# Two decoder layers on one core: list order on every engine and a fixed matmul sequence in the feed-forward part

## The chip, the cores and the metric

The kernel runs on one core of a Trainium2 chip. The metric is the device time of one execution in microseconds (us), lower is better; a timing is the median of several executions. The engines have short names in the views: PE is TensorE (matmuls), PEld its weight loads, DVE is VectorE, ACT is ScalarE, POOL is GpSimd and SP is SyncE, which here only starts DMAs. PEclk is the TensorE clock that was granted, as a share of 2.4 GHz.

## The reference

The trunk has two layers over 512 positions of width 1024, in fp32. Cut to what matters:

```python
for i in range(DEPTH):
    h = rmsnorm(x, mix_pre_g[i])
    z = h @ w_in[i]                   # columns for three mixers
    out_a = spatial_gating(...)       # causal chunks of 128
    out_b = silu(r_g) * retention(...)  # 6 heads, rotary
    out_c = forgetting_attention(...) # 6 heads, log_sigmoid(f_f + fox_b_f[i])
    x = x + rmsnorm(concat(out_a, out_b, out_c) @ w_o[i], mix_post_g[i])

    h = rmsnorm(x, ffn_pre_g[i])
    g = h @ w_gate[i]                 # 1024 x 4096
    conv = conv_b + sum(shift(g, 2 - j) * conv_w[j] for j in range(3))
    f = (gelu(conv) * (h @ w_up[i])) @ w_down[i]
    x = x + rmsnorm(f, ffn_post_g[i])

    gate = sigmoid(rmsnorm(x, ple_pre_g[i]) @ w_ple_gate[i])
    x = x + rmsnorm((p[i] @ w_ple_proj[i]) * gate, ple_post_g[i])
```

## The kernel before

Every fp32 product is made of three fp32r matmuls: each operand is split into a high and a low part (`split`: ScalarE casts the high part, VectorE subtracts it to get the low part), and TensorE adds high x high, high x low and low x high in one bank of its accumulator memory (`mm3`).

No instruction is issued where it is written. A class `Plan` records each operation with what it depends on and what it costs; `issue` then simulates the engines with those costs and with delays between engines, and so makes a list, `order`. The loop at its end (line 404, the line that every row of the profile bears) issues the operations in that order. The framework's own scheduler then orders each engine's queue, and may take operations in another order than the list's. `SETS` says how many places of 8 KB per partition the tiles of two kinds have: X for fp32r operands such as activations, W for the split feed-forward weights; raw weights (`graw`, `ws`) have no kind and go where a place is left (`pick`).

At the program's start x comes in four chunks of 128 positions. Per chunk VectorE multiplies x by the gain in two halves (`h`), TensorE transposes (`hps`), ScalarE and VectorE split the transposed tile (`hT`), and TensorE projects it (`ps`) on weights that come as `traw` and are split to `thl`.

The feed-forward part has 32 blocks of 128 columns per layer. In a block, `gate_up(b)` loads four weight pieces (`graw`: u1, u2 of w_up and g1, g2 of w_gate, one for each half of the inner dimension), makes sums of them, splits pieces and sums (`wg`, `wsa`, `wsb`, `wu`) and makes seven products in the manner of Winograd: b11 and b21 on `wg`, h6 and d on `wsa`, h7 and b22 on `wsb`, h4 on `wu`. Each is 12 matmuls of 128x256 into the banks `beta` or `ag`, and after each product ScalarE or VectorE moves the bank's values into `gs` or `us`. The convolution (`cv`), gelu and the gate follow, and a split into `act`. From block 4 on the down projection of the four blocks before is made meanwhile: 24 matmuls of 128x512 per block (`dn`), in two passes of 12, each ending in an add into `facc`. In blocks 28 to 31 there are 1, 2, 2 and 3 passes.

`down` (line 1126) is written after the whole of `gate_up` in a block, but matmuls depend only on their data, so the order of `dn` and products on TensorE follows from the list and the framework.

Of the kernel before, what the change touches and what calls it, by code (L numbers as in the profile page):

```python
# [28 lines left out]
F32R = mybir.dt.float32r  # L29
# [20 lines left out]
class Plan:  # L50
# [7 lines left out]

    SETS = {"X": 18, "W": 6}

# [7 lines left out]

    def __init__(self):
        self.ops = []  # L70
        self.table = {}
        self.tiles = {}
        self.real = {}
        self.fenced = False
        self.kind = {}
        self.place = {}
        self.scratch = bacc.Bacc("TRN2", target_bir_lowering=False, num_devices=1)

    def fence(self):

        self.fenced = True

    def pool(self, pool, psum=False):
# [63 lines left out]
    def record(self, engine, fn, method, args, kw):  # L147
# [23 lines left out]
        if engine == "PE":  # L171
            if self.fenced:
                deps.add(self.newest)
            self.newest, self.fenced = i, False
            t = self.tiles[outs[0].tensor.name]
            if len(t) > 6:
                deps.add(t[6])
            t[6:] = [i]
        self.ops.append((engine, fn, args, kw, deps, used, self.cost(engine, method, outs, ins, args, kw)))

    def cost(self, engine, method, outs, ins, args, kw):
# [13 lines left out]
        if engine == "PE":  # L195
# [3 lines left out]
            if dt == F32R:  # L199
                return 0.4416 * n + 6, 0, n * rows  # L200
            half = 0.5 if kw["lhsT"].shape[0] == 64 or kw["lhsT"].shape[-1] == 64 else 1
# [19 lines left out]
    def issue(self):  # L221
# [56 lines left out]
        def pick(t):  # L278
# [5 lines left out]
            spare, c = max(room, default=(0, None))  # L284
            return c if spare > 0 else None

# [72 lines left out]
        while len(order) < n:  # L359
# [39 lines left out]
            while finish and finish[0][0] <= now:  # L399
                _, i = heapq.heappop(finish)  # L400
                complete(i, now)
        for i in order:
            o = ops[i]
            o[1](*[self.map(v) for v in o[2]], **{k: self.map(v) for k, v in o[3].items()})  # L404

# [41 lines left out]
def packed(w):  # L447
# [16 lines left out]
    for g, u in zip(w["w_gate"], w["w_up"]):  # L464
        g, u = (blocks(m).reshape(-1, P, 2, 512) for m in (g, u))
        gu.append(np.stack([u[:, :, 1], g[:, :, 0], g[:, :, 1], u[:, :, 0]], 2))
    r["gu"] = gu
# [7 lines left out]
def body(ctx, tc, a, out):  # L475
    nc = tc.nc
    plan = Plan()
    V, A, G, T, SY = (plan.engine(n, e) for n, e in (
# [579 lines left out]
    def ffn(l, hs, emb, x, new, g, nxt):  # L1058
# [15 lines left out]

        def gate_up(b):
            raw = b8("graw", (2048,))
            load(raw, a["w_gu"][l, b].rearrange("p s n -> p (s n)"))
            u2, g1, g2, u1 = (raw[:, i * 512:i * 512 + 512] for i in range(4))
            wg = b8("wg", (2, 1024), F32R)
            split(wg[:, 0, :], wg[:, 1, :], raw[:, 512:1536])  # L1080
            s = b8("ws", (2048,))
            V.tensor_tensor(out=s[:, 512:1536].rearrange("p (s n) -> p s n", s=2), in0=raw[:, 0:1024].rearrange("p (s n) -> p s n", s=2),
                            in1=u1.unsqueeze(1).to_broadcast([P, 2, 512]), op=ALU.add)
            V.tensor_tensor(out=s[:, 0:512], in0=s[:, 1024:1536], in1=u2, op=ALU.add)
            sa = b8("wsa", (2, 1024), F32R)
            split(sa[:, 0, :], sa[:, 1, :], s[:, 0:1024])
            V.tensor_tensor(out=s[:, 1536:2048], in0=s[:, 0:512], in1=g2, op=ALU.add)
            sb = b8("wsb", (2, 1024), F32R)
            split(sb[:, 0, :], sb[:, 1, :], s[:, 1024:2048])
            wu = [wk("wu", dt=F32R) for _ in range(2)]  # L1090
            split(wu[0], wu[1], u2)

            beta, ag = bank("beta"), bank("ag")
# [16 lines left out]
            product(ga, part(sb, 1), "b22", False, True)  # L1110
            V.tensor_tensor(out=gs[:, t2], in0=ga, in1=gs[:, t2], op=ALU.add)
            product(be, wu, "h4", False, True)
            A.mul(us[:, t1], be, -1.0)

# [10 lines left out]

        def down(q, c, u):

            ps = bank("dn")
            ts = slice(c * P, c * P + P)
            for j in range(4):  # L1130
                t = acts[2 * q + j // 2]
                mm3(ps, lambda i: t[:, i, j % 2, ts], lambda i: u(i, j), j == 0, j == 3)
            return ps

        def wd(q, hf):
            return tm_units(a["w_dn"][l, q, hf], 512, 4)

        embed(l, *emb)
        for b in range(32):
            gate_up(b)  # L1140
            q, i = divmod(b, 4)
            if not q:
                continue
            i0, i1 = ((0, 2, 4, 6, 8) if q < 7 else (0, 1, 3, 5, 8))[i:i + 2]
            for hf, c in [divmod(j, 4) for j in range(i0, i1)]:
                if c == 0:
                    u = wd(q - 1, hf)
                ps = down(q - 1, c, u)
                if q == 1 and hf == 0 and c % 2 == 0:
                    facc.append(b8("facc", (2, D)))  # L1150
                fr = facc[c // 2][:, c % 2, hf * 512:hf * 512 + 512]
                if q == 1:
                    A.copy(fr, ps)
                else:
                    V.tensor_tensor(out=fr, in0=ps, in1=fr, op=ALU.add)

# [3 lines left out]
        for c in range(NCH):  # L1160
            fr = facc[c // 2][:, c % 2, :]
            parts = []
            for hf in range(2):
                ps = down(7, c, us[hf])
                cs = slice(hf * 512, hf * 512 + 512)
                V.tensor_tensor(out=fr[:, cs], in0=ps, in1=fr[:, cs], op=ALU.add)
                parts.append(post_part(fr[:, cs], g[:, 0, cs], fr[:, cs]))
# [137 lines left out]
```

## Time and profile before

| what | value |
|---|---|
| median of the 3 runs shown | 1635.08 us (1634.15 to 1640.05) |
| profiled execution | 1635.78 us |
| its span | 1633.7 us |
| its mean granted TensorE clock | 0.995 |
| TensorE busy, matmuls | 1594.8 us (98%), 10034 |
| VectorE busy | 1239.0 us (76%) |
| ScalarE busy | 840.0 us (51%) |
| GpSimd busy | 93.7 us (6%) |

The span is the time from the first to the last instruction of the profiled execution. Busy time is the time in which an engine executes, and a matmul counts as executing until its result is out, so that neighbours in a pipeline overlap; the distance between the starts of two runs of matmuls, divided by the number of matmuls, gives their true spacing.

### The profile page before, as it was taken

Reading aid. Unit: us, or ns where it says so; the run is one execution under the profiler, and the core shown is the slowest. Engines: PE = TensorE matmul, PEld = TensorE weight load, DVE = VectorE, ACT = ScalarE, POOL = GpSimd, SP = SyncE. Lnnn points to the kernel's source line nnn. Section 1 sums busy time; section 2 is a strip of 40 time slices with the busy share of each in tenths; the row PEclk is TensorE's granted clock in tenths of the full one; section 3 lists DMA queues with packets and bytes.
Section 4 is the critical chain, followed back from the end, with each engine's and each line's share of the span. In section 5 each row is a group of like instructions: output and inputs, shape, how many; then the busy total and the mean of one; then the engine's idle time right before and its main releaser. Section 6 shows DMA issues by size and latency. Waiting matters only on the chain. (4 is left out here: it accounts for less than half of the span.)

```text
span 1633.7 us, 25124 instructions
## 1 busy us (share of the span) xinstructions
PE 1594.8 (98%) x10034; PEld 1409.9 (86%) x10034; DVE 1239.0 (76%) x1949; ACT 840.0 (51%) x1378; POOL 93.7 (6%) x157
## 2 busy tenths in 40 slices
PE   6999999999999999999999999999999999999998
PEld 5887687999999999998888776879999999999987
DVE  6466758988788788786774568599788788788784
ACT  5335626765554554554562346386554554555453
POOL 1000011000000000001230000110000000000022
PEclk8999999999999999999999999999999999999999
DMA  8213216323323324336543033172334233234441
GB/s 295 91 65 104 101 69 228 108 94 114 110 78 124 104 78 129 100 99 261 192 165 104 27 129 121 49 258 78 104 104 129 78 104 129 78 104 130 179 157 65
DMA packets 63421, 197.48 MB, mean 121 GB/s; under 512 B 7348, under 2 KB 15164, under 8 KB 63304
## 3 DMA queue, kind: packets, MB, share of 16 engines
q1 hardware_dynamic: 63160, 195.81, 35.5%
q8 instruction: 79, 1.29, 0.3%
q14 instruction: 38, 0.31, 0.1%
q10 hardware_dynamic: 144, 0.07, 0.0%
HBM read 178.52 MB, written 17.33 MB: 120 GB/s over the span
## 5 line engine op out<-in xcount | busy, mean ns | idle before, releaser
L404 PE MATMUL dn<-thl,act 128*128 128x512 f32 x1536 | 368.0, 390 | 0.0
L404 PEld LDWEIGHTS dn<-thl,act 128*128 128x128 f32 x1536 | 282.8, 188 | 54.0
L404 PE MATMUL ps<-thl,hT 128*128 128x512 f32 (+3 forms) x984 | 206.5, 368 | 0.1
L404 PEld LDWEIGHTS ps<-thl,hT 128*128 128x128 f32 x984 | 177.7, 190 | 22.8 <-ACT hT L404 0.5
L404 DVE TENSOR_TENSOR thl<-traw,thl 128x1024 fp32r<-128x1024 f32 (+2 forms) x120 | 141.2, 1185 | 37.2 <-ACT thl L404 36.4
L404 ACT CAST thl<-traw 128x1024 fp32r<-128x1024 f32 (+2 forms) x120 | 121.0, 1020 | 50.6 <-PE fps L404 10.7
L404 PE MATMUL beta<-hb,wg 128*128 128x256 f32 x768 | 104.7, 281 | 4.6 <-DVE wg L404 4.6
L404 PEld LDWEIGHTS beta<-hb,wg 128*128 128x128 f32 x768 | 100.6, 189 | 9.3 <-DVE wg L404 5.0
L404 ACT COPY gs<-beta 128x256 f32<-128x256 f32 x128 | 47.6, 372 | 111.4 <-PE beta L404 111.3
L404 PE MATMUL ag<-hb,wg 128*128 128x256 f32 x768 | 103.0, 283 | 0.0
L404 PE MATMUL beta<-hh,wsa 128*128 128x256 f32 x768 | 101.7, 282 | 0.5 <-DVE wsa L404 0.2
L404 PE MATMUL beta<-hh,wu 128*128 128x256 f32 x768 | 102.0, 282 | 0.1
L404 PE MATMUL beta<-hh,wsb 128*128 128x256 f32 x768 | 101.8, 281 | 0.0
L404 PE MATMUL ag<-hd,wsa 128*128 128x256 f32 x768 | 100.8, 281 | 0.9 <-DVE gs L404 0.9
L404 PEld LDWEIGHTS beta<-hh,wu 128*128 128x128 f32 x768 | 94.0, 188 | 8.8 <-DVE us L404 7.3
L404 DVE TENSOR_TENSOR wsa<-ws,wsa 128x1024 fp32r<-128x1024 f32 x64 | 78.2, 1221 | 30.8 <-ACT wsa L404 25.7
L404 PE MATMUL ag<-hb,wsb 128*128 128x256 f32 x768 | 100.8, 280 | 0.0
L404 PEld LDWEIGHTS beta<-hh,wsa 128*128 128x128 f32 x768 | 95.4, 190 | 1.4 <-ACT gs L404 0.6
L404 PEld LDWEIGHTS ag<-hb,wg 128*128 128x128 f32 x768 | 96.3, 191 | 0.0
L404 PEld LDWEIGHTS ag<-hd,wsa 128*128 128x128 f32 x768 | 94.8, 189 | 1.7 <-DVE gs L404 1.3
L404 DVE SCALAR_TENSOR_TENSOR cv<-gs,cw,cv 128x511 f32<-128x511 f32 (+1 forms) x128 | 95.4, 745 | 0.9
L404 PEld LDWEIGHTS beta<-hh,wsb 128*128 128x128 f32 x768 | 94.5, 189 | 1.7 <-ACT gs L404 1.2
(194 smaller groups left out, 2709.1 us busy)
## 6 DMA issues: line engine op xcount, KB each, us to landing
graw<-in_w_gu_dram SPq DMA_DIRECT2D x128, 512.0 KB
traw<-in_w_dn_dram SPq DMA_DIRECT2D x64, 512.0 KB
x<-x SPq DMA_DIRECT2D x40, 512.0 KB
fraw<-in_w_fm_dram SPq DMA_DIRECT2D x30, 512.0 KB
traw<-in_w_wo_dram SPq DMA_DIRECT2D x16, 512.0 KB
traw<-in_w_pg_dram SPq DMA_DIRECT2D x16, 512.0 KB
x<-in_x_dram SPq DMA_DIRECT2D x8, 512.0 KB
traw<-in_w_uv_dram SPq DMA_DIRECT2D x8, 512.0 KB
```

The source lines that it names most:

```text
L404: o[1](*[self.map(v) for v in o[2]], **{k: self.map(v) for k, v in o[3].items()})
```

## The change

Six things change.

1. `SETS` goes from X 18 and W 6 to X 15 and W 9, and `pick` lets the oldest raw tile have a place at once.
2. `fence(True)` makes each matmul depend on the one recorded before it. It holds in the feed-forward part from block 4 to block 30, so TensorE's sequence is there the written one.
3. The cost of an fp32r matmul in the plan goes from 0.4416 n + 6 to 0.4427 n nanoseconds for n columns.
4. `issue` gives each operation a dependency without a semaphore on the operation issued before it on the same engine, so every engine, SP and GpSimd too, keeps the list's order.
5. The four weight pieces are stored in the order u2, u1, g1, g2. `wg` and `wu` are split first; then the sums are made in place in `graw` by four adds of 512 columns. Before, three adds (one of 1024 columns and two of 512) wrote to a tile of their own, `ws`. That is one 8 KB tile less and one VectorE instruction more in each of 64 blocks.
6. In a block's written order, 22 of the 24 `dn` matmuls stand between the products b22 and h4, and the last two stand after h4, at the block's end. `down` gives these two back as `rest`.

The number of matmuls stays the same, and so do the loads.

```diff
-    SETS = {"X": 18, "W": 6}
+    SETS = {"X": 15, "W": 9}
...
-    def fence(self):
+    def fence(self, always=None):
 
         self.fenced = True
+        if always is not None:
+            self.strict = always
 
...
-            if self.fenced:
+            if self.fenced or self.strict:
                 deps.add(self.newest)
...
-                return 0.4416 * n + 6, 0, n * rows
+                return 0.4427 * n, 0, n * rows
...
-            return c if spare > 0 else None
+            return c if spare > 0 or first[t] <= front else None
...
+        newest = {}
         for i in order:
             o = ops[i]
-            o[1](*[self.map(v) for v in o[2]], **{k: self.map(v) for k, v in o[3].items()})
+            made = o[1](*[self.map(v) for v in o[2]], **{k: self.map(v) for k, v in o[3].items()})
+            if o[0] in newest:
+                self.tc.add_manual_dep(made.ins, newest[o[0]], mybir.DependencyInfo(mybir.DependencyClass.NoSync, mybir.DependencyReason.DATA), reason="order of the plan")
+            newest[o[0]] = made.ins.name
...
-        gu.append(np.stack([u[:, :, 1], g[:, :, 0], g[:, :, 1], u[:, :, 0]], 2))
+        gu.append(np.stack([u[:, :, 1], u[:, :, 0], g[:, :, 0], g[:, :, 1]], 2))
...
-        def gate_up(b):
+        def gate_up(b, between):
             raw = b8("graw", (2048,))
             load(raw, a["w_gu"][l, b].rearrange("p s n -> p (s n)"))
-            u2, g1, g2, u1 = (raw[:, i * 512:i * 512 + 512] for i in range(4))
+            u2, u1, g1, g2 = (raw[:, i * 512:i * 512 + 512] for i in range(4))
             wg = b8("wg", (2, 1024), F32R)
-            split(wg[:, 0, :], wg[:, 1, :], raw[:, 512:1536])
-            s = b8("ws", (2048,))
-            V.tensor_tensor(out=s[:, 512:1536].rearrange("p (s n) -> p s n", s=2), in0=raw[:, 0:1024].rearrange("p (s n) -> p s n", s=2),
-                            in1=u1.unsqueeze(1).to_broadcast([P, 2, 512]), op=ALU.add)
-            V.tensor_tensor(out=s[:, 0:512], in0=s[:, 1024:1536], in1=u2, op=ALU.add)
-            sa = b8("wsa", (2, 1024), F32R)
-            split(sa[:, 0, :], sa[:, 1, :], s[:, 0:1024])
-            V.tensor_tensor(out=s[:, 1536:2048], in0=s[:, 0:512], in1=g2, op=ALU.add)
-            sb = b8("wsb", (2, 1024), F32R)
-            split(sb[:, 0, :], sb[:, 1, :], s[:, 1024:2048])
+            split(wg[:, 0, :], wg[:, 1, :], raw[:, 1024:2048])
             wu = [wk("wu", dt=F32R) for _ in range(2)]
             split(wu[0], wu[1], u2)
+            for t, by in ((g1, u1), (u1, u2), (u2, g1), (g2, u2)):
+                V.tensor_tensor(out=t, in0=t, in1=by, op=ALU.add)
+            sa = b8("wsa", (2, 1024), F32R)
+            split(sa[:, 0, :], sa[:, 1, :], raw[:, 0:1024])
+            sb = b8("wsb", (2, 1024), F32R)
+            split(sb[:, 0, :], sb[:, 1, :], raw[:, 1024:2048])
 
...
             product(ga, part(sb, 1), "b22", False, True)
             V.tensor_tensor(out=gs[:, t2], in0=ga, in1=gs[:, t2], op=ALU.add)
+            rest = between()
             product(be, wu, "h4", False, True)
+            if rest:
+                rest()
             A.mul(us[:, t1], be, -1.0)
...
-        def down(q, c, u):
+        def down(q, c, u, done):
 
             ps = bank("dn")
             ts = slice(c * P, c * P + P)
             for j in range(4):
                 t = acts[2 * q + j // 2]
-                mm3(ps, lambda i: t[:, i, j % 2, ts], lambda i: u(i, j), j == 0, j == 3)
-            return ps
+                for i, (h, r) in enumerate(((0, 0), (0, 1), (1, 0))):
+                    if j < 3 or not i:
+                        T.matmul(ps, lhsT=t[:, h, j % 2, ts], rhs=u(r, j), start=j == 0 and i == 0, stop=False)
+
+            def rest():
+                T.matmul(ps, lhsT=t[:, 0, 1, ts], rhs=u(1, 3), start=False, stop=False)
+                T.matmul(ps, lhsT=t[:, 1, 1, ts], rhs=u(0, 3), start=False, stop=True)
+                done(ps)
+            return rest
 
         def wd(q, hf):
             return tm_units(a["w_dn"][l, q, hf], 512, 4)
 
-        embed(l, *emb)
-        for b in range(32):
-            gate_up(b)
+        units = {}
+
+        def pieces(b):
+
             q, i = divmod(b, 4)
             if not q:
-                continue
+                return None
+            rest = None
             i0, i1 = ((0, 2, 4, 6, 8) if q < 7 else (0, 1, 3, 5, 8))[i:i + 2]
             for hf, c in [divmod(j, 4) for j in range(i0, i1)]:
                 if c == 0:
-                    u = wd(q - 1, hf)
-                ps = down(q - 1, c, u)
+                    units[q, hf] = wd(q - 1, hf)
                 if q == 1 and hf == 0 and c % 2 == 0:
                     facc.append(b8("facc", (2, D)))
-                fr = facc[c // 2][:, c % 2, hf * 512:hf * 512 + 512]
-                if q == 1:
-                    A.copy(fr, ps)
-                else:
-                    V.tensor_tensor(out=fr, in0=ps, in1=fr, op=ALU.add)
+
+                def add(ps, fr=facc[c // 2][:, c % 2, hf * 512:hf * 512 + 512]):
+                    if q == 1:
+                        A.copy(fr, ps)
+                    else:
+                        V.tensor_tensor(out=fr, in0=ps, in1=fr, op=ALU.add)
+                if rest:
+                    rest()
+                rest = down(q - 1, c, units[q, hf], add)
+            return rest
+
+        embed(l, *emb)
+        for b in range(31):
+            if b == 4:
+                plan.fence(True)
+            gate_up(b, lambda: pieces(b))
+        plan.fence(False)
+        gate_up(31, lambda: None)
+        pieces(31)()
 
...
-                ps = down(7, c, us[hf])
                 cs = slice(hf * 512, hf * 512 + 512)
-                V.tensor_tensor(out=fr[:, cs], in0=ps, in1=fr[:, cs], op=ALU.add)
+                down(7, c, us[hf], lambda ps: V.tensor_tensor(out=fr[:, cs], in0=ps, in1=fr[:, cs], op=ALU.add))()
```

How the instructions move shows in the order on the engines' queues; xN is a number of like instructions in a row.

VectorE at the program's start, before. `h` is x times the gain, two per chunk; `thl` 128x1024 is the split of the first weights, `thl` 128x2x390 that of the `fv` weights, `hT` the low part of the transposed h.

```order
L404 TENSOR_TENSOR h<-x,gain 128x512 x2
L404 TENSOR_TENSOR thl<-traw,thl 128x1024
L404 TENSOR_TENSOR hT<-hps,hT 128x4x128 x2
L404 TENSOR_TENSOR thl<-traw,thl 128x1024 x3
L404 TENSOR_TENSOR thl<-traw,thl 128x2x390 x2
L404 TENSOR_TENSOR h<-x,gain 128x512 x5
L404 TENSOR_TENSOR hT<-hps,hT 128x4x128 x3
L404 TENSOR_TENSOR h<-x,gain 128x512
L404 TENSOR_TENSOR hT<-hps,hT 128x4x128 x2
```

The same place on VectorE with the change:

```order
L408 TENSOR_TENSOR h<-x,gain 128x512 x2
L408 TENSOR_TENSOR thl<-traw,thl 128x1024
L408 TENSOR_TENSOR hT<-hps,hT 128x4x128 x2
L408 TENSOR_TENSOR thl<-traw,thl 128x1024 x3
L408 TENSOR_TENSOR h<-x,gain 128x512 x5
L408 TENSOR_TENSOR hT<-hps,hT 128x4x128 x3
L408 TENSOR_TENSOR h<-x,gain 128x512
L408 TENSOR_TENSOR hT<-hps,hT 128x4x128 x2
L408 CAST ang<-posi 128x512
L408 TENSOR_SCALAR ang<-ang,invf 128x512
L408 TENSOR_SCALAR angn<-ang 128x512
L408 TENSOR_TENSOR hT<-hps,hT 128x4x128
```

The two splits of the `fv` weights stood ahead of the five `h` and now stand behind these rows.

TensorE in one block of layer 1's feed-forward part, before, from the product b11 (`hb` on `wg`) to the block's last `dn`:

```order
L404 MATMUL beta<-hb_2154,wg 128x256 x12
L404 MATMUL ag<-hb_2169,wg 128x256 x12
L404 MATMUL beta<-hh_2239,wsa 128x256 x12
L404 MATMUL ag<-hd,wsa 128x256 x12
L404 MATMUL beta<-hh_2248,wsb 128x256 x12
L404 MATMUL ag<-hb_2228,wsb 128x256 x12
L404 MATMUL dn<-thl,act 128x512 x2
L404 MATMUL beta<-hh_2266,wu 128x256 x12
L404 MATMUL dn<-thl,act 128x512 x22
```

The same in each block with the change:

```order
L408 MATMUL beta<-hb_2154,wg 128x256 x12
L408 MATMUL ag<-hb_2169,wg 128x256 x12
L408 MATMUL beta<-hh_2237,wsa 128x256 x12
L408 MATMUL ag<-hd,wsa 128x256 x12
L408 MATMUL beta<-hh_2252,wsb 128x256 x12
L408 MATMUL ag<-hb_2275,wsb 128x256 x12
L408 MATMUL dn<-thl,act 128x512 x22
L408 MATMUL beta<-hh_2295,wu 128x256 x12
L408 MATMUL dn<-thl,act 128x512 x2
```

The run of 22 `dn` and the run of two have changed places around the seventh product; before, other blocks had other runs at other places, and now all from 4 to 27 are alike.

ScalarE ahead of layer 1's output projection, before. `fet` is a copy of transposed attention weights out of `tps`, `rr` a step of the same mixer, the casts to `thl` are splits of weights, those to `ehl` and `cc` other operands.

```order
L404 COPY fet<-tps 128x4x128
L404 ACTIVATE rr<-rps 32x512
L404 CAST thl<-traw 128x1024
L404 COPY rr<-rps 32x512
L404 ACTIVATE rr<-rps 32x512
L404 COPY rr<-rps 32x512
L404 CAST thl<-traw 128x1024
L404 COPY fet<-tps 128x4x128
L404 CAST ehl<-eraw 128x1024
L404 CAST cc<-ops 128x512
```

The same place on ScalarE with the change:

```order
L408 COPY fet<-tps 128x4x128
L408 ACTIVATE rr<-rps 32x512
L408 COPY rr<-rps 32x512
L408 COPY fet<-tps 128x4x128
L408 ACTIVATE rr<-rps 32x512
L408 COPY rr<-rps 32x512
L408 CAST cc<-ops 128x512
L408 CAST thl<-traw 128x1024 x6
```

The casts of weights have moved behind both copies to `fet`.

## Rows read from the trace of the kernel before

**Rows 1.** The page: busy time, share of the span and instructions of each engine.
```profile
PE 1594.8 (98%) x10034; PEld 1409.9 (86%) x10034; DVE 1239.0 (76%) x1949; ACT 840.0 (51%) x1378; POOL 93.7 (6%) x157
```

**Rows 2.** Windows, three stretches: the two at the start, then blocks 5 to 27.
```profile
core 0: us, PE busy (x) PEld busy (x) DVE busy (x) ACT busy (x) POOL busy (x), PEclk, DMA share, GB/s
17.70:25.50 7.80, 0.01 (x1) 0.01 (x1) 2.60 (x4) 4.84 (x7) 0.79 (x2) 0.68 0.98 306
25.50:30.00 4.50, 4.50 (x21) 4.50 (x22) 4.50 (x7) 3.09 (x5) 1.18 (x1) 0.50 1.01 395
335.80:691.00 355.20, 355.14 (x2486) 329.95 (x2485) 291.46 (x386) 186.26 (x283) 0.00 (x0) 1.00 0.31 101
```

**Rows 3.** Timeline of PE, blocks 5 and 6: start, duration, group, idle before and releaser.
```profile
336.10 1.58 PE L404 MATMUL beta<-hb,wg 128*128 128x256 f32 x12
...
340.34 0.39 PE L404 MATMUL dn<-thl,act 128*128 128x512 f32 x1
340.57 1.53 PE L404 MATMUL ag<-hd,wsa 128*128 128x256 f32 x12
...
346.01 5.40 PE L404 MATMUL dn<-thl,act 128*128 128x512 f32 x23
351.25 1.58 PE L404 MATMUL beta<-hb,wg 128*128 128x256 f32 x12
...
359.73 0.63 PE L404 MATMUL dn<-thl,act 128*128 128x512 f32 x2
360.20 1.53 PE L404 MATMUL beta<-hh,wu 128*128 128x256 f32 x12
361.56 5.17 PE L404 MATMUL dn<-thl,act 128*128 128x512 f32 x22
```

**Rows 4.** Timeline of PE, the first product of block 28.
```profile
691.32 1.58 PE L404 MATMUL beta<-hb,wg 128*128 128x256 f32 x12
```

**Rows 5.** Timeline of DVE at the program's start.
```profile
12.84 2.35 DVE L404 TENSOR_TENSOR thl<-traw,thl 128x1024 fp32r<-128x1024 f32 x2
22.78 2.06 DVE L404 TENSOR_TENSOR thl<-traw,thl 128x780 fp32r<-128x780 f32 x2 [7.59 <-ACT thl L404]
24.75 3.54 DVE L404 TENSOR_TENSOR h<-x,gain 128x512 f32<-128x512 f32 x5
...
30.61 1.27 DVE L404 TENSOR_TENSOR hT<-hps,hT 128x512 fp32r<-128x512 f32 x2
```

**Rows 6.** Timeline of ACT at the program's start.
```profile
13.38 1.06 ACT L404 ACTIVATE junk<-x 128x1024 bf16<-128x1024 f32 x1 [0.15 <-DMA x<-in_x_dram]
...
19.77 1.05 ACT L404 ACTIVATE junk<-x 128x1024 bf16<-128x1024 f32 x1
...
21.90 0.84 ACT L404 CAST thl<-traw 128x780 fp32r<-128x780 f32 x1 [0.99 <-DMA traw<-in_w_fv_dram]
```

**Rows 7.** Timeline of PE at the program's start.
```profile
25.49 4.53 PE L404 MATMUL hps<-k_ident,h 128*128 128x128 f32 x20 [7.83 <-DVE h L404]
29.67 1.92 PE L404 MATMUL ps<-thl,hT 128*128 128x512 f32 x5
```

**Rows 8.** Timeline of PE, the end of a later block.
```profile
406.11 0.39 PE L404 MATMUL dn<-thl,act 128*128 128x512 f32 x1
406.47 1.66 PE L404 MATMUL beta<-hh,wu 128*128 128x256 f32 x12
407.96 5.40 PE L404 MATMUL dn<-thl,act 128*128 128x512 f32 x23
```

**Rows 9.** Lines of DVE, blocks 5 to 27: count, busy us, mean ns, idle before.
```profile
L404 DVE TENSOR_TENSOR ws<-ws,graw 128x512 f32<-128x512 f32 x46 | 31.6, 687 | 0.8
...
L404 DVE TENSOR_TENSOR ws<-graw 128x1024 f32<-128x1024 f32 x22 | 26.8, 1218 | 0.3
```

**Rows 10.** Timeline of PE, the first products of layer 1's feed-forward part.
```profile
278.62 1.42 PE L404 MATMUL beta<-hb,wg 128*128 128x256 f32 x10 [2.28 <-DVE wg L404]
```

**Rows 11.** Timeline of PE ahead of layer 1's output projection.
```profile
204.38 2.37 PE L404 MATMUL ops<-fet,mix 128*64 128x512 f32 x14 [1.78 <-ACT fet L404]
```

**Rows 12.** Timeline of PE, the same place in layer 2.
```profile
1008.30 2.37 PE L404 MATMUL ops<-fet,mix 128*64 128x512 f32 x14 [2.06 <-ACT fet L404]
```

More of the change, by code (lines that the diff above doesn't have):

```diff
@@ L67, with __init__ @@
     HOP_PE = {"PE": 0, "DVE": 250, "ACT": 270, "POOL": 190, "SP": 100}
-    def __init__(self):
+    def __init__(self, tc):
+        self.tc = tc
         self.ops = []
@@ L73, in __init__ @@
         self.real = {}
-        self.fenced = False
+        self.fenced = self.strict = False
         self.kind = {}
@@ L476, in body @@
     nc = tc.nc
-    plan = Plan()
+    plan = Plan(tc)
     V, A, G, T, SY = (plan.engine(n, e) for n, e in (
```

## The prediction

> **What bounds the kernel now.** I read the page first. TensorE is busy for 98% of the span, VectorE for 76% [rows 1]. A busy share that high can still hide time, because a matmul that is spaced more widely than it need be counts as busy. So the next view was the windows, by stage: at the program's start TensorE stands idle from 17.70 to 25.50 and then runs 4.5 us at a granted clock of 0.50, the lower of its two levels (1.2 GHz); in blocks 5 to 27 of layer 1's feed-forward part it is busy for 355.14 of 355.20 us at clock 1.00 [rows 2]. The bound of the feed-forward part is therefore TensorE's own spacing of matmuls, and the third view, the timeline with start times, shows that spacing.
>
> In the timeline of the feed-forward part a run's start is exact enough to divide by. Block 5 starts at 336.10 and block 28 at 691.32 [rows 3, 4]: 355.22 / 23 = **15.44 us per block**. Inside, the same 128x256 matmul has two spacings. After one `dn` matmul at 340.34, 48 of them take 340.57 to 346.01, 113.3 ns each; after 23 `dn`, 72 take 351.25 to 359.73, 117.8 ns each; after two `dn` again, 12 take 360.20 to 361.56, 113.3 ns [rows 3]. All are at clock 1.00 and nothing waits. Over both layers I found 20 runs of one or two `dn` with no wait behind them, and all are followed by the 113 ns spacing; 54 runs of twelve or more `dn` are all followed by 118 ns. I don't know the mechanism; I take the regularity as it stands.
>
> **The start: list order on VectorE.** Now VectorE ends the splits of the first weights at 12.84 + 2.35 = 15.19, then idles 7.59 us, because the split of the `fv` weights stands next in its queue, and those land late: ScalarE starts on them at 21.90, released by their DMA [rows 5, 6]. Behind it stand five `h` (x times gain), which TensorE's transposes need; its idle time ends on them at 25.49, and chunk 1's projection starts at 29.67 [rows 7]. The x that they read was there: ScalarE reads chunk 1 at 13.38, and the last chunk at the latest at 19.77 [rows 6]. After the change the five `h` stand ahead of that split. They run from 15.19 for 3.54 us to 18.7, two low parts of hT add 1.27, so the projection starts near 20.0: 29.67 − 20.0 = 9.7 us earlier. The lower bound is the idle time alone, 7.6. I take **−9**: the transposes, now 4.53 us at the lower clock, come after a shorter pause, but the DMA engines are 98% busy in that stretch [rows 2], and later weights may not keep pace.
>
> **The feed-forward part: where the `dn` stand.** The new block runs six products, 22 `dn`, the seventh product and two `dn`. By the regularity the six products follow a run of two and the seventh a run of 22: 72 x 113.3 ns = 8.16, 12 x 117.8 = 1.41, and 24 `dn` at (351.25 − 346.01) / 23 = 227.8 ns = 5.47. Sum **15.04 us** against 15.44: −0.40 x 23 = −9.2 per layer. Blocks 28 to 31 also begin behind a run of two: 4 x 72 x 4.5 ns = −1.3. Two layers: **−21**.
>
> Part of that is not spacing. In 12 blocks per layer the seventh product waits for its weights `wu`, which VectorE splits last: 406.11 to 406.47 is 0.36 for one `dn`, 0.13 too much, and the product takes 1.49, where 12 x 117.8 would be 1.41 and 12 x 113.3 is 1.36 [rows 8]; in all 0.21 to 0.26 us, about 5 us over 24 blocks. After the change `wu` is split ahead of the sums and has 22 `dn`, 5 us, in front of its product, so these waits should go. The other 16 are spacing.
>
> The Trainium skill, "TensorE: Matmul & The Clock Gate", section "Back-to-back issue gap", gives the isolated gap of a warm matmul as set by its column count alone, N/2.4 + 2.5 ns with 262 cycles for N = 256; by it the order of runs would change nothing. The trace disagrees, with 113.3 and 117.8 ns for one shape [rows 3]; by the page this term would keep only its 5 us of waits.
>
> **The price of a fixed sequence.** Now the scheduler may put a `dn` where a product's operand isn't ready, as at 340.34 between `wsa` and `d` [rows 3]. After the change nothing can be put there: a product that waits holds all behind it, 24 `dn` and the next block's products. At each of four boundaries a ScalarE or VectorE step that drains the bank must fit under the product between. Such a step has 12 x 113.3 = 1.36 us now instead of 1.41. The trace has no row of a fixed sequence; below, the price is nothing, above it is one wait of 0.21 at each of four boundaries in 28 blocks of two layers, 0.21 x 4 x 56 = +47. I take **+2**, near the lower end, because in block 5's neighbour (351.25 to 359.73) six products already run in that sequence without a gap.
>
> **Sums in place.** Per block one add of 1218 ns and two of 687 [rows 9] make 2.59 us; four of 687 make 2.75, +0.16. VectorE is busy 291.46 / 23 = 12.67 us per block [rows 2], then 12.83 of 15.04: 2.2 us stay free, and that hides it. Without that cover it would be 0.16 x 64 = 10 us. The sums now stand behind the splits of `wg` and `wu`, so `wsa` comes later relative to its load, while one 8 KB tile per block is saved. At a layer's entry the first `wg` product waits 2.28 us on VectorE's split [rows 10]; `wg` no longer stands behind the adds, `wsa` does. I take **0**, bounds −4.6 and +4.6: the 2.28 us gone or doubled in both layers.
>
> **List order elsewhere, tile sets.** In the mixers the output projection waits 1.78 and 2.06 us on a ScalarE copy `fet` [rows 11, 12], ahead of which the old queue has casts of weights; the new queue has both `fet` copies first. **−3**, bounds 0 and −3.8. SP's loads, too, now go in list order: a load that waits for its buffer holds the later ones, while the DMA engines are 31% busy in the feed-forward part [rows 2], which hides some delay. Three fewer X places and three more W places, the cost constants and POOL's order have no row; I take 0, bounds −6 and +6: the two mixer waits and the entry wait (1.78 + 2.06 + 2.28) saved or met once more.
>
> **Sum.** −9 − 21 + 2 − 3 = −31. The profiled execution took 1635.8 us (span 1633.7), 0.7 over the median of the runs shown, so 1604.8 by it and 1604.1 by the median: I say **1605**.
>
> **Rivals.**
> A: the spacing doesn't follow the last run of `dn` but something that goes along with it in the old order, such as which product comes next. For it: I have no mechanism. Against: 20 of 20 and 54 of 54. Then the 16 us of spacing stay: **1621**.
> B: the start is gained and lost again, because the `fv` weights and those after them land no earlier and TensorE waits for them instead. For it: the DMA engines are 98% busy before 25.5 [rows 2], and `fv` lands at 21.90 [rows 6]. Against: the first weights are split by 15.19 [rows 5], and three more chunks can be projected on them. Then −9 becomes 0: **1614**.
> C (slower): waits at the boundaries of the fixed sequence. For it: VectorE has but 2.2 us per block free, and its work comes in bursts. With 0.21 us at all four boundaries the time is 1605 − 2 + 47 = **1650**. It decides from 40 us on, 0.7 us per block in 56 blocks: then the time is over 1643.
> D: list order helps in more places of the mixers and at the layers' entries, since other queues too hold a late load's split ahead of ready work. Both lower bounds above, −6 and −4.6: **1594**.
> E: no net change, by the mechanism of C at two or three of the four boundaries: 0.21 x 2.5 x 56 = 29 us eat the gains, **1632**. That the change doesn't do what it says is excluded by the rows of the order shown with the change.
>
> **How the numbers follow.** The forecast as summed has 0.48, A 0.13, B 0.12, C 0.06, D 0.15, E 0.06. A difference under 0.5%, 8.2 us, can't be told from none. The range goes from D's value, 1594, to just above A, 1622; outside stand C, E and the half of D that gains more than its value, 0.2 in all. The likeliest case alone, with small errors in its four terms, has 1598 to 1612. Faster by over 0.5% (under 1626.9) are the forecast, A, B and D: 0.88; the same is E, 0.06; slower is C, 0.06.
>
> **What would show it.** Right: block starts 15.0 us apart; 113 ns in six products and 118 in the seventh; no wait ahead of `wu`; VectorE's gap of 7.6 us at the start gone and the projection near 20; the `fet` wait under 0.5. Wrong: 118 ns in all products (A); a gap on `fv` or `fm` weights before 60 us (B); repeated gaps of 0.2 us ahead of `h6`, `h7` or `b22` named on ScalarE or VectorE (C). The forecast rests above all on two matmuls of `dn` at a block's end setting the spacing of the next 72.

## The result and the profile after

The changed kernel takes 1615.36 us (median of 4 runs, 1614.30 to 1617.16) against 1636.64 for the kernel before in the same comparison: a ratio of 0.987, 95% interval 0.9847 to 0.9892. That is 21 us less where 31 were forecast. The profiled execution took 1614.30 us, its span is 1612.5, its granted clock 0.998.

The page of the changed kernel, busy time by engine:

```profile
PE 1577.5 (98%) x10034; PEld 1393.0 (86%) x10034; DVE 1240.0 (77%) x2013; ACT 840.5 (52%) x1380; POOL 92.0 (6%) x157
```

TensorE's share is 98% as before [rows 1], with the same 10034 matmuls in 17 us less: they lie closer together. VectorE has the 64 instructions more and hardly more busy time.

To see where the time went I cut both traces at the starts of the same matmuls: the first `sps` (attention scores), the first `wo` (output projection), the first `beta` (feed-forward part) and the last `dn` of each layer. Each length is the distance between two such starts, the first one from the start of the span; the last column is an experiment told below.

| stage, us | before | changed | X 18, W 6 |
|---|---|---|---|
| program start to `sps` | 74.1 | 64.0 | 64.9 |
| `sps` to `wo`, layer 1 | 126.2 | 129.7 | 127.0 |
| `wo` to `beta`, layer 1 | 75.4 | 76.0 | 75.4 |
| `beta` to last `dn`, layer 1 | 501.2 | 489.6 | 490.1 |
| last `dn` to `wo`, layer 2 | 227.0 | 230.4 | 227.8 |
| `wo` to `beta`, layer 2 | 75.7 | 76.0 | 75.4 |
| `beta` to last `dn`, layer 2 | 500.6 | 492.3 | 490.5 |
| last `dn` to last matmul | 46.1 | 47.0 | 46.1 |

The changed kernel gains 10.0 us at the start and 11.6 + 8.3 = 19.9 in the two feed-forward parts, and gives back 3.5 and 3.4 in the two stages with attention, 0.8 around the output projections and 0.9 at the end: 8.6 in all.

The changed kernel's timeline of VectorE at the program's start:

```profile
15.14 3.10 DVE L408 TENSOR_TENSOR h<-x,gain 128x512 f32<-128x512 f32 x5
...
20.54 1.29 DVE L408 TENSOR_TENSOR hT<-hps,hT 128x512 fp32r<-128x512 f32 x2
```

Where it idled 7.59 us [rows 5], the five `h` now start at 15.14, right behind the splits of the first weights. On TensorE one chunk's projection on the first weights is 24 matmuls `ps`. Before, chunk 0's ran without a break, and TensorE then stood idle up to 25.49 [rows 7]:

```profile
9.87 7.80 PE L404 MATMUL ps<-thl,hT 128*128 128x512 f32 x24
```

In the changed kernel the transposes of the later chunks stand among them:

```profile
9.90 6.50 PE L408 MATMUL ps<-thl,hT 128*128 128x512 f32 x17
16.25 0.60 PE L408 MATMUL hps<-k_ident,h 128*128 128x128 f32 x4
16.60 0.48 PE L408 MATMUL ps<-thl,hT 128*128 128x512 f32 x1
...
19.05 2.33 PE L408 MATMUL ps<-thl,hT 128*128 128x512 f32 x9
```

Behind the 17 come three single ones (16.60, 17.71, 18.38) and four of the nine; the 25th, with which chunk 1 begins, starts at 20.07 where it was 29.67 [rows 7]. A view of the trace from 20.24 on, when chunk 0's last one has ended, begins with it:

```profile
20.07 1.31 PE L408 MATMUL ps<-thl,hT 128*128 128x512 f32 x5
```

The changed kernel's timeline of TensorE from there on, in the order of time:

```profile
194.17 2.37 PE L408 MATMUL ops<-fet,mix 128*64 128x512 f32 x14
...
212.73 0.66 PE L408 MATMUL cps<-k_ident,ro 128*128 128x128 f32 x4 [1.07 <-DVE ro L408]
...
224.09 0.63 PE L408 MATMUL cps<-k_ident,ro 128*128 128x128 f32 x4 [0.61 <-DVE ro L408]
...
271.95 1.42 PE L408 MATMUL beta<-hb,wg 128*128 128x256 f32 x10 [1.78 <-DVE wg L408]
...
277.17 0.50 PE L408 MATMUL beta<-hh,wsa 128*128 128x256 f32 x2 [1.65 <-ACT wsa L408]
...
328.95 1.53 PE L408 MATMUL beta<-hb,wg 128*128 128x256 f32 x12
...
359.33 1.53 PE L408 MATMUL beta<-hb,wg 128*128 128x256 f32 x12
...
367.50 5.17 PE L408 MATMUL dn<-thl,act 128*128 128x512 f32 x22
372.51 1.58 PE L408 MATMUL beta<-hh,wu 128*128 128x256 f32 x12
373.92 0.63 PE L408 MATMUL dn<-thl,act 128*128 128x512 f32 x2
374.39 1.53 PE L408 MATMUL beta<-hb,wg 128*128 128x256 f32 x12
...
675.59 1.53 PE L408 MATMUL beta<-hb,wg 128*128 128x256 f32 x12
...
1565.10 0.97 PE L408 MATMUL ps<-thl,hT 128*128 128x512 f32 x3 [1.72 <-DVE thl L408]
```

Read it from the middle. A block runs from 359.33 to 374.39, 15.06 us: six products in 367.50 − 359.33 = 8.17, 113.5 ns a matmul, and the seventh, behind 22 `dn`, in 373.92 − 372.51 = 1.41, 117.5 ns. Over blocks 5 to 27 it is (675.59 − 328.95) / 23 = 15.07 us against 15.44 [rows 3, 4]. At the entry the wait on `wg`, 2.28 [rows 10], is 1.78, and a wait of 1.65 on `wsa` has come behind it. The wait on `fet` [rows 11] is gone (194.17), but some 19 and 30 us later the projection's neighbours `cps` wait 1.07 and 0.61 on `ro`. At 1565.10, in the last embedding stage, a wait of 1.72 on weights is new.

What no wait shows is the loss between `sps` and `wo`. TensorE has 128.55 us of work in 129.6 there, and its idle time is 0.7 us less than before. Grouped by shape, the attention's matmuls that fill only half of the array (64 rows for the scores `sps`, 64 columns for `ops`) have the same counts and more busy time. (A shape in a row names the rows and columns of the array, then the result; one such matmul of the program is two records in the trace, which accounts for the counts.) Lines of PE between `sps` and `wo` of layer 1, before: count, busy us, mean ns, idle before.

```profile
L404 PE MATMUL sps<-fqk 64*128 64x384 f32 x12 | 3.4, 508 | 0.0
L404 PE MATMUL ops<-fet,mix 128*64 128x512 f32 x10 | 3.4, 618 | 0.1
L404 PE MATMUL sps<-fqk 64*128 64x512 f32 x12 | 3.2, 606 | 0.0
...
L404 PE MATMUL ops<-fet,mix 128*64 128x384 f32 x8 | 1.8, 486 | 0.0
```

And the same lines of the changed kernel:

```profile
L408 PE MATMUL ops<-fet,mix 128*64 128x512 f32 x10 | 5.4, 618 | 0.3 <-ACT fet L408 0.3
L408 PE MATMUL sps<-fqk 64*128 64x512 f32 x12 | 4.4, 624 | 0.0
L408 PE MATMUL sps<-fqk 64*128 64x384 f32 x12 | 4.2, 500 | 0.0
L408 PE MATMUL ops<-fet,mix 128*64 128x384 f32 x8 | 3.3, 499 | 0.0
```

One matmul takes as long as before (618 ns for `ops` 128x512, before and after), but the group covers 5.4 us instead of 3.4: the matmuls overlap less. The starts tell why. Two `sps` 64x384 side by side alternate: their starts lie 6, 316, 7 and 316 ns apart, 645 ns for both. Where another matmul stands between the two, the one by itself takes 323 + 412 = 735 ns. The new order on TensorE has such places (here a shape is that of the result in the program, so that `ops` 64x512 is the pair of records 128x512 above):

```
L408 MATMUL fps<-hT,fhl 128x512
L408 MATMUL ops<-fet,mix_414 64x512
L408 MATMUL fps<-hT,fhl 128x512 x2
L408 MATMUL ops<-fet,mix_414 64x512
L408 MATMUL ops<-fet,mix_414 64x384 x2
```

Before, the two `ops` 64x512 stood in one row of the order, and so did both `sps` of a pair with 384 columns. Summed from each start to the next matmul's start, `ops` and `sps` take 14.3 us in this stage before and 18.1 after. The difference of 3.8 covers the stage's loss of 3.5. Between the layers, in the next attention, they take 15.4 and 18.1: 2.7 of the 3.4 lost there.

### The profile page after: what moved, and what is told of

Its sections match the earlier page's. It is cut to its first block, busy times and chain, and to the rows that moved or that the text cites. A ratio compares the mean times of both kernels' runs of the same rounds, so it can differ in the third digit from the quotient of the medians.

```text
span 1612.5 us, 25222 instructions
## 1 busy us (share of the span) xinstructions
PE 1577.5 (98%) x10034; PEld 1393.0 (86%) x10034; DVE 1240.0 (77%) x2013; ACT 840.5 (52%) x1380; POOL 92.0 (6%) x157
## 5 line engine op out<-in xcount | busy, mean ns | idle before, releaser
L408 DVE TENSOR_TENSOR graw<-graw 128x512 f32<-128x512 f32 x256 | 176.3, 690 | 2.7
L408 PEld LDWEIGHTS beta<-hh,wu 128*128 128x128 f32 x768 | 98.3, 189 | 6.1 <-DVE us L408 1.9
L408 PE MATMUL beta<-hb,wg 128*128 128x256 f32 x768 | 99.8, 278 | 3.6 <-DVE wg L408 3.6
L408 DVE TENSOR_TENSOR wg<-graw,wg 128x1024 fp32r<-128x1024 f32 x64 | 78.3, 1224 | 28.0 <-PE beta L408 17.7
L408 PE MATMUL beta<-hh,wsa 128*128 128x256 f32 x768 | 98.2, 277 | 1.7 <-ACT wsa L408 1.6
L408 DVE TENSOR_TENSOR wsb<-graw,wsb 128x1024 fp32r<-128x1024 f32 x64 | 78.3, 1224 | 27.2 <-PE beta L408 18.2
L408 PE MATMUL beta<-hh,wsb 128*128 128x256 f32 x768 | 98.2, 277 | 0.0
```

Source lines behind the costliest of these rows:

```text
L408: made = o[1](*[self.map(v) for v in o[2]], **{k: self.map(v) for k, v in o[3].items()})
```

## The experiments

Every comparison is against the kernel before on the same chip; its median was 1636.3 in the first two groups of four and 1633.8 in the third (X 18, W 6 with the old cost; the sums with X 18, W 6; the run without the fixed sequence; the last one). The changed kernel itself ran beside a kernel before of 1636.6, so against the third group the ratios are the fairer measure.

**Where the last down matmuls stand.** Three kernels change one number, how many `dn` are left for a block's end (`TAIL` is 0, 3 or 4 in place of 2; the code is cut):

```diff
-                    if j < 3 or not i:
+                    if 3 * j + i < 12 - TAIL:
...
             def rest():
-                T.matmul(ps, lhsT=t[:, 0, 1, ts], rhs=u(1, 3), start=False, stop=False)
-                T.matmul(ps, lhsT=t[:, 1, 1, ts], rhs=u(0, 3), start=False, stop=True)
+                for m in range(12 - TAIL, 12):
+                    ...
```

None:

> All 24 down matmuls of a block stand ahead of the seventh product, none at the block's end. Theory (the last run of down matmuls sets the spacing): the six products that follow have 118 ns, 72 x 4.5 ns = 0.32 us more per block, in some 54 blocks +17.5 us: 1633. Rival (the place in the block, or which product it is, sets the spacing): 113 ns stay in six products, 1615 as the changed kernel.

Three:

> Three instead of two down matmuls at a block's end. The trace of the changed kernel has four runs of three, each followed by 113 ns, so the theory says 113 ns in six products and 1615, within 2 us. Rival (two is special): 118 ns and 1633.

Four:

> Four down matmuls at a block's end. The trace of the changed kernel has two runs of four, each followed by 60 matmuls at 118 ns. Theory (a run long enough loses the short spacing, and four is long enough): 118 ns in all products, 1633. Rival (any tail at the block's end will do, and those two places were something else): 1615.

Measured: none 1632.24 us (ratio to before 0.9973, 0.9964 to 0.9983), three 1617.83 (0.9883, 0.9864 to 0.9902), four 1635.33 (0.9991, 0.9980 to 1.0001). All three are nearest to what the theory said and far from the rival, though not exactly: three came 2.8 us over its 1615, where 2 had been allowed, and four 2.3 over its 1633. The timelines of TensorE in one block, first with none at the end:

```profile
405.63 1.58 PE L408 MATMUL beta<-hh,wu 128*128 128x256 f32 x12
407.05 1.58 PE L408 MATMUL beta<-hb,wg 128*128 128x256 f32 x12
...
415.53 2.68 PE L408 MATMUL dn<-thl,act 128*128 128x512 f32 x11
```

84 matmuls from 405.63 to 415.53, 117.9 ns each. With three:

```profile
404.13 0.86 PE L408 MATMUL dn<-thl,act 128*128 128x512 f32 x3
404.83 1.52 PE L408 MATMUL beta<-hb,wg 128*128 128x256 f32 x12
...
412.99 4.95 PE L408 MATMUL dn<-thl,act 128*128 128x512 f32 x21
```

72 matmuls from 404.83 to 412.99, 113.3 ns. With four:

```profile
421.12 1.09 PE L408 MATMUL dn<-thl,act 128*128 128x512 f32 x4
422.05 1.58 PE L408 MATMUL beta<-hb,wg 128*128 128x256 f32 x12
...
424.88 1.58 PE L408 MATMUL beta<-hh,wsa 128*128 128x256 f32 x12
426.63 1.65 PE L408 MATMUL ag<-hd,wsa 128*128 128x256 f32 x12 [0.18 <-DVE gs L408]
428.12 1.52 PE L408 MATMUL beta<-hh,wsb 128*128 128x256 f32 x12
```

24 matmuls from 422.05 to 424.88, 117.9 ns; then a wait on VectorE, and after it 113 ns. So two or three `dn` at a block's end give the short spacing to the products behind them, and none or four do not. The tail is worth 1632.24 − 1615.36 = 17 us; the prediction had put 16 on spacing.

It is not simply a matter of how long the run is. At the end of a layer, where the blocks are no longer alike, the run with four has five `dn` in a row, and the short spacing is back behind them:

```profile
732.04 1.32 PE L408 MATMUL dn<-thl,act 128*128 128x512 f32 x5
733.20 1.54 PE L408 MATMUL beta<-hh,wsa 128*128 128x256 f32 x12
...
740.02 0.86 PE L408 MATMUL dn<-thl,act 128*128 128x512 f32 x3
```

60 matmuls from 733.20 to 740.02, 113.7 ns. Such a run of five stands in both layers of this kernel and of the one with none, each time with 113.6 to 113.8 ns behind it.

**List order.** Left out of the changed kernel (the code is cut):

```diff
-            if o[0] in newest:
-                self.tc.add_manual_dep(made.ins, newest[o[0]], ...)
-            newest[o[0]] = made.ins.name
```

> The dependency on the operation issued before it on the same engine is left out; the fixed sequence, the tail and the sums in place stay. Theory (list order gains at the start and is about even elsewhere): VectorE's idle gap of 7.6 us at the start comes back and the time is 1621 to 1623, all of it ahead of the first output projection. Rival (list order loses in the mixers what it gains at the start): 1615 or less, later at the start and earlier behind it.

Measured 1625.37 us (0.9930, 0.9911 to 0.9949), 10 more than the changed kernel and 2 more than expected. VectorE's gap is back in this run's timeline:

```profile
23.05 2.05 DVE L408 TENSOR_TENSOR thl<-traw,thl 128x780 fp32r<-128x780 f32 x2 [7.71 <-ACT thl L408]
25.02 3.56 DVE L408 TENSOR_TENSOR h<-x,gain 128x512 f32<-128x512 f32 x5
```

The stage from the start to `sps` takes 74.0 us in it, 9.9 more than in the changed kernel. List order put alone into the kernel before is the same three lines added:

> The kernel before with list order on every engine and nothing else. Theory (list order is worth some 10 us at the start, as leaving it out cost, and little elsewhere): 1626. Rival (list order loses in the mixers and in the feed-forward part what it gains at the start): 1632 to 1640.

Measured 1619.45 us (0.9895, 0.9879 to 0.9908): 17 less than before, 7 more gain than I expected. Its stage to `sps` is 64.3 us, so the start gives 9.8, nearly as in the changed kernel. The rest comes from the feed-forward parts, 497.8 and 498.4 us against 501.2 and 500.6, and from attention, 124.2 us in layer 1 against 126.2; the output projections take 0.7 to 1.0 more each. The theory was right about the start and wrong that nothing else would move.

**The places.** One line:

```diff
-    SETS = {"X": 15, "W": 9}
+    SETS = {"X": 18, "W": 6}
```

> Only SETS goes back to X 18 and W 6; all else as in the changed kernel. By the stages of the traces the changed kernel without list order needs 3.7 us more than before from the start to the first output projection, and 3.3 us more from layer 1's last down matmul to layer 2's output projection. Theory (fewer X places delay the mixers): these 7 us come back, 1608. Rival 1 (the places don't bind, the cost constant set another order): 1615. Rival 2 (six W places are too few for the fixed sequence): waits on wsa, wsb or wu in the blocks, 1617 or more.

Measured 1605.93 us (0.9812, 0.9792 to 0.9832): 9 less than the changed kernel, and the fastest of all the kernels. By the table of stages 2.7 us come back in each of two stages with attention, 1.2 around the projections, 1.3 in the feed-forward parts and 0.9 at the end, and 0.9 is lost at the start. In its order some of the half-array matmuls are next to their neighbours again (`ops` and `sps` together 16.1 us, against 18.1). The places bind, as the theory said, and the six for W did not starve the fixed sequence. The new cost of a matmul, undone alone:

```diff
-                return 0.4427 * n, 0, n * rows
+                return 0.4416 * n + 6, 0, n * rows
```

> Only the plan's cost of an fp32r matmul goes back to 0.4416 n + 6. Theory (the 7 us outside the feed-forward part come from the places): 1615. Rival (they come from the order that the new cost gives): 1608.

Measured 1618.47 us (0.9891, 0.9874 to 0.9908), 3 more than the changed kernel; attention keeps its loss (130.2 us in layer 1), so the rival fell. Both undone together:

> X 18 and W 6, and the matmul cost 0.4416 n + 6 in the plan, as before; all else as in the changed kernel. The mixers of the kernel before with list order took 2.8 and some 5 us less than those with X 18 and W 6 under the new cost. Theory (the old cost gives the mixers a better order): 1599 to 1603. Rival (costs shift the order at random, as the 3 us that the old cost lost alone): 1604 to 1609.

Measured 1615.49 us (0.9879, 0.9857 to 0.9901). The theory failed: attention did take 124.2 us in layer 1, as expected (`ops` and `sps` 14.1 us, all pairs whole), but the feed-forward parts went to 495.7 and 496.3 us, with eight waits of 0.2 to 1.2 us in the first blocks of layer 1. Two edits worth −9 and +3 alone give about 0 together (by the ratios 0.9879 against 0.9870, a loss of 1.5).

All fourteen kernels sort by these two numbers. With X 15 and W 9, `ops` and `sps` take 18.1 us in layer 1 and the stage 129.7 to 130.2, whatever else is changed, list order left out and the old cost included. With X 18, W 6 and the new cost it is 16.1 and 127, with the old cost 14.1 to 14.3 and 124.2 to 126.2. So the plan's numbers set how the pairs stand.

**The sums.** In a tile of their own again, as before the change, behind the splits of `wg` and `wu` (shortened: `wsa` and `wsb` are then split from `s`, and the last add stands behind the split of `wsa`):

```diff
-            for t, by in ((g1, u1), (u1, u2), (u2, g1), (g2, u2)):
-                V.tensor_tensor(out=t, in0=t, in1=by, op=ALU.add)
+            s = b8("ws", (2048,))
+            V.tensor_tensor(out=s[:, 512:1536]..., in0=(u2, g1), in1=u1 twice, op=ALU.add)
+            V.tensor_tensor(out=s[:, 0:512], in0=s[:, 1024:1536], in1=u2, op=ALU.add)
+            V.tensor_tensor(out=s[:, 1536:2048], in0=s[:, 0:512], in1=g2, op=ALU.add)
```

> The weight sums go to a tile of their own again, with one add of 1024 and two of 512 columns, behind the splits of wg and wu; the rest as in the changed kernel. Theory (the one add more is hidden, and so is the tile): 1615, within 2 us. Rival (the in-place sums free the places that the fixed sequence needs): waits at the products on wsa and wsb, 1620 or more.

Measured 1623.77 us (0.9922, 0.9905 to 0.9939), 8 more: the theory fell. In this run's timeline of TensorE the wait at the entry is longer, and one stands in a block of the steady part:

```profile
273.12 1.87 PE L408 MATMUL beta<-hb,wg 128*128 128x256 f32 x10 [2.84 <-DVE wg L408]
...
379.60 0.50 PE L408 MATMUL beta<-hh,wsa 128*128 128x256 f32 x2 [0.64 <-ACT gs L408]
380.58 1.43 PE L408 MATMUL beta<-hh,wsa 128*128 128x256 f32 x10 [0.48 <-DVE wsa L408]
```

Is that the three places that X lost, or the tile as such? The same edit with X 18 and W 6:

> X 18 and W 6 as before, and the weight sums in a tile of their own. With X 15 and W 9 the tile of its own cost 8.4 us. Theory 1 (the tile and the add cost by themselves, whatever the places): 1606 + 8 = 1614. Theory 2 (the in-place sums only pay for the three X places that the raw weights can't have any more): 1606, within 2 us.

Measured 1614.93 us (0.9880, 0.9855 to 0.9906), 9.0 more than with the sums in place and the same places (1605.93). So the gain of the in-place sums doesn't depend on the places: theory 1. The two times are from two groups of runs; in the group of the slower one the kernel before was 2.6 us faster, so the groups don't make the difference. Whether the tile or the order of the loads costs it isn't settled; by the stages 4 to 6 of the 8 to 9 us stand in the feed-forward parts and 3 to 4 between the layers.

**The fixed sequence.** Left out, with the written order and the tail kept:

```diff
-            if b == 4:
-                plan.fence(True)
```

> The changed kernel without the fixed matmul sequence; the written order, the tail of two, list order and the sums in place stay. Theory (the fixed sequence is what keeps two down matmuls at a block's end, and costs next to nothing): the list breaks the runs in part of the blocks, the short spacing is lost there, and the time is 1617 to 1630. Rival (the fixed sequence costs waits, and the written order alone would do): 1605 to 1613.

Measured 1613.73 us (0.9870, 0.9847 to 0.9893), the same ratio to the kernel before as the changed kernel's 0.987. Here the theory fell, and the rival's gain didn't come either: 46 blocks still have a run of two and 72 matmuls at 113 ns behind it, so the written order and list order are enough for that. The feed-forward parts take 490.2 and 491.4 us, the changed kernel's 489.6 and 492.3.

**One more short run.** The kernel with X 18, W 6 and the old cost, with four `dn` held back and two of them put after three matmuls of the seventh product:

```diff
-            product(be, wu, "h4", False, True)
+            product(be, wu, "h4", False, True, range(1))
             if rest:
-                rest()
+                rest(2)
+            product(be, wu, "h4", False, True, range(1, 4))
+            if rest:
+                rest(2)
```

> As the run with X 18, W 6 and the old cost, but two down matmuls more are held back: 20 down matmuls, three of the seventh product, two, the other nine of the product, two. Theory (a short run of down matmuls resets the spacing wherever it stands): the nine go from 118 to 113 ns, 9 x 4.5 ns x 54 blocks = 2.2 us less than that run. Rival (three matmuls between two runs of down matmuls are too few to end a run): nothing gained, or the spacing of the whole block is lost, 16 us more.

Measured 1614.79 us against 1615.49 without (0.9876, 0.9850 to 0.9901, against 0.9879). Its timeline of TensorE:

```profile
355.46 0.52 PE L408 MATMUL beta<-hh,wu 128*128 128x256 f32 x3
355.81 0.63 PE L408 MATMUL dn<-thl,act 128*128 128x512 f32 x2
356.28 1.19 PE L408 MATMUL beta<-hh,wu 128*128 128x256 f32 x9
357.31 0.63 PE L408 MATMUL dn<-thl,act 128*128 128x512 f32 x2
357.77 0.62 PE L408 MATMUL beta<-hb,wg 128*128 128x256 f32 x4
```

The nine matmuls take 1.03 us, 114 ns each, so three matmuls are enough between two runs, and a short run does reset the spacing there. But each run of two costs (356.28 − 355.81) / 2 = 235 ns a matmul where a long run has 228, which takes back a third, and 0.7 us in all is less than the measurement can tell.

## Why the prediction was right, and where its sum was off

The time lies in the range, and two thirds of the way from before: 21 us of a forecast 31. By the stages, the start and the feed-forward parts gave 29.9 where 28 were forecast (−9 − 21 + 2); everything else lost 8.6 where 3 were to be gained. So the two main steps were right, and the miss lies in the terms for what stands around them. That the time is still in the range owes something to luck: it is above 1612, the end of the likeliest case, and so inside only by the room left for rivals A and B. It is also within 2 us of B's 1614, though what B said did not happen.

**The start, −9: right.** It gave 10.0 in the changed kernel and 9.8 with list order alone. The five `h` moved as worked out, and chunk 1's projection begins at 20.07, worked out as near 20.0. Rival B, a loss to the next late weights, did not happen: TensorE waits for no weights up to the first `sps`.

**The feed-forward part, −21 + 2: right.** It gave 19.9. A block takes 15.07 us, worked out as 15.04, and the tail's count decides it as the regularity said, with what the trace of before could not show, that four is too many and five is not. Rival A is excluded by the runs with none and with four. The isolated gap that the Trainium skill gives by the column count alone ("TensorE: Matmul & The Clock Gate", "Back-to-back issue gap") does not agree with these runs: one shape has 113.3 and 117.9 ns by the number of `dn` ahead of it.

**The price of a fixed sequence, +2: small as forecast, but it is nothing.** Rival C's waits did not come: in blocks 5 to 27 of layer 1 TensorE waits for nobody. But leaving the fixed sequence out moves nothing either: the written order and list order make the sequence.

**The output projection, −3: wrong.** The wait on `fet` went, and the same stage lost as much again to `cps` waiting on `ro`: 75.4 became 76.0. The step took one wait's end for the stage's end; I should have asked what the projection waits for next. Nor was it list order that ended this wait: the changed kernel without it has no wait on `fet` in the projection either, and its stage takes 75.0, while list order alone in the kernel before gives 76.4.

**Sums in place, 0: wrong.** "2.2 us stay free, and that hides it" holds for VectorE's add, but the step priced only the add. With X 15 and W 9 the sums in place are worth 8.4 us, with X 18 and W 6 9.0.

**"List order elsewhere, tile sets": wrong, and the largest miss.** "I take 0, bounds −6 and +6" stands against 7.8 us more, 7 between `sps` and `wo` of layer 1 and between the layers and 0.9 at the end, so even the bound was too narrow. X 15 and W 9 cost 9.4 us here, since X 18 and W 6 give them back (2 to 3 with the old cost). In layer 1 the overlap of half-array matmuls accounts for that in size: over four orders `ops` and `sps` took 14.1, 14.3, 16.1 and 18.1 us where the stage took 124.2, 126.2, 127.0 and 129.7. No run changed the pairing alone, so this cause is read from the traces, not shown by itself. The step priced the tile sets in waits saved or met; a busy engine with fewer overlaps was not on its list, though the pair's split stood in the order. Taken out one at a time the tail is worth 17 us, list order 10, the sums in place 8.4 and the places −9.4; these don't add up to 21, so the terms act on each other, which a plain sum can't show.

The kernel with X 18 and W 6, 1605.93 us, is to be preferred to both. That it stands at the forecast of 1605 is no merit of the forecast, which gave the places no price.

## What to carry to other kernels

Divide the distance of two starts by the count, shape by shape: an engine that is 98% busy had 17 us in the spacing of its matmuls, and two instructions moved to a block's end gave them back. When a planner's numbers change, compare the order also where nothing was edited, and look there at busy groups and not at waits alone: a pair that overlaps costs when something is put between. Try such numbers each by itself and together, since a −9 and a +3 made about 0 here.

## What the runs showed of the hardware

The spacing of 128x256 matmuls depends on the run of 128x512 matmuls ahead of them, at the same granted clock of 1.00. Over the traces of all fourteen kernels, counting the runs with no irregular spacing in them (over 240 ns) or right behind them (over 125 ns): one to three are followed by 113 to 114 ns (674 of 675 runs), four by 117.9 (76 of 76), five by 113.6 to 113.8 (4 of 4), eight or more by 117.9 (688 of 688). So it is no threshold in the length. The spacing stayed for all of the 72 or 84 matmuls up to the next run, unless a pause came between; a short one was enough. In the kernel before with list order, one spacing of 165 ns at 694.24 us turned 118 ns into 113 without any `dn`. The 128x512 matmuls change too: the first five in a run are 228 to 236 ns apart, the later ones 227. Why, stays open.

Half-array matmuls overlap with a neighbour of the same kind: two `sps` 64x384 side by side took 645 ns together, one by itself 735. One full-array matmul between them ends the overlap, and no wait shows it.
